# Gate outputs and three chunks of h transposed by 32x32 blocks on the vector engine, in a hybrid decoder layer

## The chip, the core and the metric

One core of a Trainium2 chip runs the whole layer as one program. The metric is device time in microseconds (us). The kernel before took 1821.63 us, the median of three runs (1821.47 to 1821.71). The engines are named as the profile names them: PE is TensorE (PEld its weight loads), DVE is VectorE, ACT is ScalarE, POOL is GpSimd, SP is SyncE, which only issues transfers here.

## The reference

A decoder layer over 256 tokens of width 2048, in fp32: a half-weighted SwiGLU feed-forward, a mixer of two head groups, a second feed-forward, a last norm.

```
h = x
h = h + 0.5 * swiglu(rmsnorm(h, ffn1_norm), w_gate, w_up, w_down)     # 2048 -> 5504 -> 2048
hn = rmsnorm(h, mix_norm);  q, k, v, u = split(hn @ w_in)
mixed = concat(rmsnorm(s5_mixer(u)), rmsnorm(dilated_attention(q, k, v)))
h = h + mixed @ w_out
h = h + 0.5 * swiglu(rmsnorm(h, ffn2_norm), w_gate, w_up, w_down)
return rmsnorm(h, final_norm)

swiglu(x) = (silu(x @ w_gate) * (x @ w_up)) @ w_down
```

## The kernel before

**Products.** Tokens lie on partitions, in two blocks of 128 (NTB = 2). Every product takes its left operand transposed (features on partitions, 256 tokens along the row) and its weights as they lie in memory. Both are kept as two fp32r halves, an upper one (the rounded value) and a lower one (the rest), and each product is the sum of three matmuls, xh*wh + xh*wl + xl*wh (mm3, L92 to L96, 128x512 each). `product` (L98) walks over the contraction in weight blocks of four k-tiles (1 MB, issued by SP, three buffers), and each block in two half blocks of two k-tiles: `halves` (L82) makes whi by a copy on ACT (L88) and wlo by a subtraction on DVE (L89), with four buffers of each, then 2 k-tiles x 2 token blocks x 3 matmuls follow. After each half block the next deferred closures of `self.soon` are called, and `step` (L175) draws one piece of background work from `self.later`. In the first feed-forward this is `prepare` (L627): tables of powers and of E for the state space, then eight groups (`ssm_groups`, L515), four yields each.

**Feed-forward.** `ffn` (L266) walks over 11 chunks of 512 columns (the last has 384): a gate product G, an up product U (8 half blocks each), then per token block a silu on ACT (L282), a product with U on DVE (L283, into one of two silu buffers), and a deferred `transpose_split` (L136): four 128x128 transposes on PE into PSUM (L142), a copy to the upper half on ACT (L146) and a subtraction for the lower half on DVE (L147). The result is a pair xh, xl that the down projection reads: four chunks of h, 22 half blocks each (L289 to L295).

**A finished chunk of h.** In the first feed-forward and in the second half of the mixer's output projection (L912 to L923, 4 half blocks for each chunk), `finish_chunk` (L250) defers the eight transposes of that chunk of h (with its gain, so that ACT and DVE split 128x128 pieces one by one, L151 and L152) and adds its squares to the statistics. The next product over h needs the pairs, one for each of its weight blocks.

**Start.** `setup` puts 12 matmuls on zeros in front (L203). The first gate product works in smaller pieces (`opening`, L104): x comes already transposed from memory and is split beside the weights (`split_x`, L229).

**End.** The last chunk of h is normed and stored (L931 to L945); `probe` (L947) issues 24 matmuls on zero tiles in between, whose results nobody reads.

**Order.** No queue is written out by hand. Tile's scheduler orders the instructions of each engine: the program's order is the priority, an instruction that is not ready by its plan is passed by others, and each engine then executes its list in the order so fixed. 32 slots of 4 KB per partition hold most tiles.

Of the kernel before, what the change touches and what calls it, by code (L numbers as in the profile page):

```python
# [4 lines left out]

# [4 lines left out]
F32 = mybir.dt.float32  # L10
F32R = mybir.dt.float32r
AF = mybir.ActivationFunctionType
# [19 lines left out]
class Layer:  # L32
# [4 lines left out]
    def __init__(self, ctx, tc, ins, out):  # L37
        self.tc, self.nc, self.t, self.out = tc, tc.nc, ins, out
        pool = lambda name, bufs, **kw: ctx.enter_context(tc.tile_pool(name=name, bufs=bufs, **kw))
        self.const = pool("const", 1)  # L40
        self.wpool = pool("weights", 2)
        self.slots = pool("slots", NSLOT)
        self.work = pool("work", 2)
        self.psum = pool("psum", 1, space=PSUM)
        self.dram = pool("scratch", 1, space=DRAM)
        self.n = 0
        self.later = deque()
        self.soon = deque()
        self.fetch = None


# [46 lines left out]
    def product(self, accs, xT, w, r0, nkt, c0, n, tail=0):  # L98


        held = []
        for k0 in range(0, nkt, 4):
            nk = min(4, nkt - k0)
            opening = self.fetch is not None and self.xraw is not None and k0 == 0  # L104
            raw = self.wraw(w, r0 + k0 * P, nk, c0, n, (1, 1, 2) if opening else (4,))
            if self.fetch is not None:
                self.fetch(k0 // 4 + 1)
            xh, xl = xT[k0 // 4]
            for kk, ke in ((0, 1), (1, 2), (2, 4)) if opening else ((0, 2), (2, 4)):
                ke = min(ke, nk)  # L110
                if kk >= ke:
                    continue
                if self.fetch is not None:
                    self.split_x(k0 + kk, k0 + ke)
                wh, wl = self.halves(raw[:, kk:ke, :n])
                for k in range(kk, ke):
                    for tb in range(NTB):
                        ts = slice(tb * P, (tb + 1) * P)
                        mm = partial(
                            self.mm3, accs[tb][:, :n], xh[:, k, ts], xl[:, k, ts], wh[:, k - kk, :n],  # L120
                            wl[:, k - kk, :n], k0 + k == 0, k0 + k == nkt - 1,
                        )
                        if tb and k0 + 4 * tail >= nkt:
                            held.append(mm)
                        else:
                            mm()
                while self.soon and k0 + kk >= 2:
                    self.soon.popleft()()
                self.step()
        for mm in held:  # L130
            mm()
# [4 lines left out]
    def transpose_split(self, pair, src, tb, nt, gain=None):  # L136

        nc = self.nc
        hi, lo = pair
        ps = self.trp()  # L140
        for k in range(nt):
            nc.tensor.transpose(ps[:, k * P : (k + 1) * P], src[:, k * P : (k + 1) * P], self.ident)  # L142
        ts = slice(tb * P, (tb + 1) * P)
        if gain is None:
            psv = ps[:, : nt * P].rearrange("p (k t) -> p k t", t=P)
            nc.scalar.activation(hi[:, :nt, ts], psv, AF.Copy)  # L146
            nc.vector.tensor_sub(lo[:, :nt, ts], psv, hi[:, :nt, ts].bitcast(F32))  # L147
        else:
            for k in range(nt):
                pk = ps[:, k * P : (k + 1) * P]  # L150
                nc.scalar.activation(hi[:, k, ts], pk, AF.Copy, scale=gain[:, k : k + 1])  # L151
                nc.vector.scalar_tensor_tensor(  # L152
                    lo[:, k, ts], pk, gain[:, k : k + 1], hi[:, k, ts].bitcast(F32),
                    op0=ALU.mult, op1=ALU.subtract,
                )

    def stat(self, nchunk):
        return [
# [29 lines left out]
    def setup(self):  # L188
        nc, t = self.nc, self.t
        self.gains = self.const.tile([P, 64], F32, name="gains")  # L190
        nc.scalar.dma_start(self.gains, t["gains"])
        self.g_ffn1, self.g_mix, self.g_ffn2 = (self.gains[:, 16 * i : 16 * i + 16] for i in range(3))
        self.g_ssm, self.g_att = (self.gains[:, 48 + 8 * i : 56 + 8 * i] for i in range(2))
        self.h = self.const.tile([P, NTB, D_MODEL], F32, name="h")
        self.ident = self.const.tile([P, P], F32, name="ident")
        self.even = self.const.tile([P, 3], F32, name="even")
        self.mhalf = self.even[:, 2:3]

        warm = self.slot([P, 512], F32R, s="warm")
        nc.vector.memset(warm.bitcast(F32), 0.0)  # L200
        idle = self.acc("idle")
        for _ in range(12):
            nc.tensor.matmul(idle, warm[:, :P], warm, start=True, stop=True)  # L203
        self.xraw = {}
        self.xT = [None] * 4
        self.st = self.stat(4)

        def fetch(c):
            if c == 2 and self.xraw is None:
                for tb in range(NTB):  # L210
                    nc.sync.dma_start(self.h[:, tb], t["x"][tb])
                nc.gpsimd.dma_start(self.ident, t["mask"][:, 3 * P : 4 * P])
                nc.gpsimd.dma_start(self.even, t["mask"][:, 4 * P :])
                self.later.appendleft(self.first_squares())
            if c > 3 or self.xT[c] is not None:
                return
            self.xraw[c] = raw = self.slot([P, 4, SEQ], s="xraw")
            self.xT[c] = self.pair()
            if c:
                self.fetch_x(c, 0, 4)  # L220

        self.r = None
        self.fetch = fetch
        fetch(0)
# [25 lines left out]
    def finish_chunk(self, c, gain):  # L250

        self.xT[c] = pair = self.pair()
        hs = [self.h[:, tb, c * 512 : (c + 1) * 512] for tb in range(NTB)]

        def transposes():
            for tb in range(NTB):
                self.transpose_split(pair, hs[tb], tb, 4, gain[:, 4 * c : 4 * c + 4])

        self.soon.append(transposes)
        for tb in range(NTB):  # L260
            self.square(self.st[tb], c, hs[tb], 512)

# [3 lines left out]
    def ffn(self, wg, wu, wd, finish, tail=0):  # L266
        nc = self.nc
        gT = []
        for c0, n in FCH:
            G = [self.acc("g") for _ in range(NTB)]  # L270
            self.product(G, self.xT, wg, 0, 16, c0, n)
            self.xraw = None
            U = [self.acc("u") for _ in range(NTB)]
            self.product(U, self.xT, wu, 0, 16, c0, n)
            if self.fetch is not None:
                self.fetch = None
                self.norms()
            pair = self.pair()
            gT.append(pair)
            for tb in range(NTB):  # L280
                s = self.tmp([P, 512], "silu", 2)
                nc.scalar.activation(s[:, :n], G[tb][:, :n], AF.Silu, scale=self.r[tb])  # L282
                nc.vector.scalar_tensor_tensor(  # L283
                    s[:, :n], U[tb][:, :n], self.r[tb], s[:, :n], op0=ALU.mult, op1=ALU.mult
                )
                self.soon.append(partial(self.transpose_split, pair, s, tb, n // P))
        self.xT = [None] * 4
        self.st = self.stat(4)
        for c in range(4):  # L289
# [636 lines left out]
    def ffn2(self):  # L926
# [1 line left out]
        self.gfin = None  # L928
        self.ffn(t["ffn2_w_gate"][0], t["ffn2_w_up"][0], t["ffn2_w_down"][0], self.last_chunk, 2)
        out = self.out  # L930
        self.probe()  # L931
        for tb in range(NTB):
            r = self.tmp([P, 1], "rstd", 6)
            nc.vector.tensor_scalar(r, self.st[tb][:, 3:4], 1.0 / D_MODEL, self.part[tb], op0=ALU.mult, op1=ALU.add)
# [9 lines left out]
                    nc.scalar.activation(hs, hs, AF.Copy, scale=r)  # L944
                (nc.sync if c % 2 else nc.scalar).dma_start(out[tb, :, cs], hs)  # L945

    def probe(self):  # L947

        z, zb = self.idle
        mm = partial(self.nc.tensor.matmul, start=True, stop=True)  # L950
        p = [self.trp("idle") for _ in range(2)]
        for i in range(4):
            mm(p[0], z[:, :P], z)
        for i in range(4):
            mm(p[0], z[:, i * P : (i + 1) * P], z)
        for i in range(4):
            mm(p[0], zb[:, i * P : (i + 1) * P], zb[:, :512])
        for i in range(4):
            mm(p[0][:64], z[:, i * P : i * P + 64], z)
        for i in range(4):  # L960
            mm(p[i % 2], z[:, i * P : (i + 1) * P], z)
        for i in range(4):
            mm(p[0][:, :256], z[:, i * P : (i + 1) * P], z[:, :256])

    def last_chunk(self, c):
        nc = self.nc
        if c == 2:
            self.idle = self.slot([P, 512], F32R, s="z"), self.slot([P, 512], mybir.dt.bfloat16, s="zb")
            nc.gpsimd.memset(self.idle[0].bitcast(F32), 0.0)
            nc.gpsimd.memset(self.idle[1], 0.0)  # L970
        if self.gfin is None:
            gf = self.t["final_norm"].rearrange("(o d) -> o d", o=1)
            self.gfin = [self.slot([P, 512], s="gfin") for _ in range(4)]
# [83 lines left out]
```

## Time and profile before

| | |
|---|---|
| median of three runs | 1821.63 us |
| the profiled execution | 1820.6 us |
| its span, first to last instruction | 1818.7 us |
| PE busy | 1810.3 us |
| DVE busy | 1033.5 us |
| ACT busy | 862.1 us |
| granted clock | 1.00 |

The profile is of one execution. Busy time is the union of the instructions of an engine; matmuls are pipelined, so that one of them shows about 390 ns while the next starts 227 ns later. A line of the timeline gives the start, the time that it covers, the engine, the line of the code, what is written from what, and in brackets the idle time before it and what ended it.

### The profile page before, as it was taken

What the parts mean: (1) busy time and instruction counts of PE and PEld (TensorE: products, weight loads), DVE (VectorE), ACT (ScalarE), POOL (GpSimd) and SP (SyncE); (2) the same over time, 40 slices, a digit from 0 to 9 for tenths busy, and PEclk for the clock granted to TensorE, in tenths of its full rate; (3) what the DMA queues carried; (4) which work ended last, traced back from release to release, by engine and by line L of the source; (5) the groups of instructions that cost most, each with busy time, mean ns of one, the idle gap of its engine ahead of it and who ended that gap; (6) DMA issues with size and microseconds to landing.
All of it is one profiled execution on the core that took longest, in us unless ns stands there. A gap on an engine that the chain in (4) does not pass through costs nothing.

```text
span 1818.7 us, 21868 instructions
## 1 busy us (share of the span) xinstructions
PE 1810.3 (100%) x8514; PEld 1519.8 (84%) x8515; DVE 1033.5 (57%) x1532; ACT 862.1 (47%) x1205; POOL 91.5 (5%) x175
## 2 busy tenths in 40 slices
PE   9999999999999999999999999999999999999999
PEld 7888888888988888888888888888888888988887
DVE  5796688545445544566666565544555544544553
ACT  6544567444444444443368555444444444444443
POOL 2102022500000000000000000000000000000000
PEclk9999999999999999999999999999999999999999
DMA  8667667855555557676544455555555555755553
GB/s 322 201 213 239 206 244 248 282 186 184 187 197 190 192 189 259 214 264 242 161 139 139 139 176 191 189 185 186 192 194 191 185 186 171 224 198 183 207 191 121
DMA packets 180327, 364.16 MB, mean 200 GB/s; under 512 B 8256, under 2 KB 17344, under 8 KB 179968
## 3 DMA queue, kind: packets, MB, share of 16 engines
q1 hardware_dynamic: 172192, 343.96, 56.6%
q0 software_dynamic: 6736, 16.69, 2.7%
q10 hardware_dynamic: 1296, 2.13, 0.4%
q8 instruction: 66, 1.08, 0.2%
q14 instruction: 37, 0.30, 0.0%
HBM read 346.36 MB, written 16.38 MB: 199 GB/s over the span
## 4 chain that ended last, share of the span: by engine, by line
PE 99%; DMA 1%; SPq 0%; DVE 0%; ACT 0%; issue 0%
PE u L94 9%; PE u L96 9%; PE y L96 9%; PE u L95 9%; PE y L95 9%; PE y L94 9%; PE g L95 9%; PE g L96 9%; PE g L94 8%; PE pr L94 3%; PE pr L96 3%; PE pr L95 3%; PE tr L142 2%; PE wo L94 2%; PE wo L96 2%; PE wo L95 2%
## 5 line engine op out<-in xcount | busy, mean ns | idle before, releaser
L89 DVE TENSOR_TENSOR wlo<-wraw,whi 128x1024 fp32r<-128x1024 f32 (+2 forms) x633 | 760.3, 1203 | 715.1 <-ACT whi L88 714.2
L88 ACT ACTIVATE whi<-wraw 128x1024 fp32r<-128x1024 f32 (+2 forms) x633 | 659.1, 1043 | 845.3 <-PE y L96 258.0
L94 PE MATMUL g<-whi,xh 128*128 128x512 f32 (+1 forms) x704 | 272.6, 388 | 2.0 <-ACT xh L237 1.5
L95 PE MATMUL g<-wlo,xh 128*128 128x512 f32 (+1 forms) x704 | 270.8, 385 | 1.1 <-DVE wlo L89 1.1
L94 PE MATMUL u<-whi,xh 128*128 128x512 f32 (+1 forms) x704 | 270.7, 385 | 0.0
L96 PE MATMUL g<-whi,xl 128*128 128x512 f32 (+1 forms) x704 | 270.5, 385 | 0.0
L96 PE MATMUL u<-whi,xl 128*128 128x512 f32 (+1 forms) x704 | 270.4, 384 | 0.0
L95 PE MATMUL u<-wlo,xh 128*128 128x512 f32 (+1 forms) x704 | 270.3, 384 | 0.0
L94 PE MATMUL y<-whi,xh 128*128 128x512 f32 x688 | 268.1, 390 | 0.0
L96 PE MATMUL y<-whi,xl 128*128 128x512 f32 x688 | 267.7, 389 | 0.0
L95 PE MATMUL y<-wlo,xh 128*128 128x512 f32 x688 | 267.7, 389 | 0.0
L94 PEld LDWEIGHTS g<-whi,xh 128*128 128x128 f32 x704 | 132.0, 188 | 27.8 <-ACT xh L237 2.2
L95 PEld LDWEIGHTS g<-wlo,xh 128*128 128x128 f32 x704 | 132.2, 188 | 26.3 <-DVE wlo L89 1.9
L96 PEld LDWEIGHTS g<-whi,xl 128*128 128x128 f32 x704 | 132.1, 188 | 25.0
L95 PEld LDWEIGHTS u<-wlo,xh 128*128 128x128 f32 x704 | 132.2, 188 | 24.9
L96 PEld LDWEIGHTS u<-whi,xl 128*128 128x128 f32 x704 | 132.1, 188 | 25.0
L94 PEld LDWEIGHTS u<-whi,xh 128*128 128x128 f32 x704 | 132.1, 188 | 24.8
L95 PEld LDWEIGHTS y<-wlo,xh 128*128 128x128 f32 x688 | 129.2, 188 | 26.9
L96 PEld LDWEIGHTS y<-whi,xl 128*128 128x128 f32 x688 | 129.1, 188 | 26.7
L94 PEld LDWEIGHTS y<-whi,xh 128*128 128x128 f32 x688 | 129.1, 188 | 26.6
L94 PE MATMUL pr<-whi,xh 128*128 128x512 f32 x256 | 101.9, 398 | 0.0
L96 PE MATMUL pr<-whi,xl 128*128 128x512 f32 x256 | 100.2, 391 | 0.0
(221 smaller groups left out, 1450.1 us busy)
## 6 DMA issues: line engine op xcount, KB each, us to landing
wraw<-in_ffn_w_up SPq DMA_DIRECT2D x80, 1024.0 KB, 5.1
wraw<-in_ffn_w_down SPq DMA_DIRECT2D x80, 1024.0 KB, 5.0
wraw<-in_ffn_w_gate SPq DMA_DIRECT2D x79, 1024.0 KB, 5.1
wraw<-in_w_in SPq DMA_DIRECT2D x32, 1024.0 KB, 5.6
wraw<-in_w_out SPq DMA_DIRECT2D x16, 1024.0 KB, 5.0
wraw<-in_ffn_w_gate SPq DMA_DIRECT2D x8, 768.0 KB, 4.4
wraw<-in_ffn_w_up SPq DMA_DIRECT2D x8, 768.0 KB, 4.4
wraw<-in_ffn_w_down SPq DMA_DIRECT2D x8, 768.0 KB, 4.3
```

The source lines that it names most:

```text
L88: nc.scalar.activation(hi[:, :nk, :n], raw, AF.Copy)
L89: nc.vector.tensor_sub(lo[:, :nk, :n], raw, hi[:, :nk, :n].bitcast(F32))
L94: nc.tensor.matmul(out, xh, wh, start=first, stop=False)
L95: nc.tensor.matmul(out, xh, wl, start=False, stop=False)
L96: nc.tensor.matmul(out, xl, wh, start=False, stop=last)
L142: nc.tensor.transpose(ps[:, k * P : (k + 1) * P], src[:, k * P : (k + 1) * P], self.ident)
```

## The change

The transposes of all gate outputs and of the first three chunks of h (in both places that call `finish_chunk`) leave PE. `turn_split` takes a raw tile and defers 32 transposes on DVE: each takes 32 partitions of one token block, with four (three in the narrow chunk) 32x32 blocks along the row, and writes them turned to another group of 32 partitions. A last entry splits the whole into halves. `product` calls three entries of the list after each half block, and all that are left of a pair before the weight block that reads it. The first gate product is put under `manual_schedule`, so that its instructions are issued in the order written. The warm-up has 10 matmuls, the probe and its zero tiles go.

```diff
@@ product
+            while any(x is xT[k0 // 4] for x, _ in self.turns):
+                self.turns.popleft()[1]()
             xh, xl = xT[k0 // 4]
@@ product, after the matmuls of a half block
                 while self.soon and k0 + kk >= 2:
                     self.soon.popleft()()
+                for _ in range(min(3, len(self.turns))):
+                    self.turns.popleft()[1]()
                 self.step()
@@
+    def turn_split(self, pair, src, nt, gain=None):
+        nc = self.nc
+        hi, lo = pair
+        raw = self.slot([P, 4, SEQ], s="turned")
+
+        def turn(tb, a, b):
+            nc.vector.transpose(
+                raw[32 * b : 32 * b + 32, :nt, tb * P + 32 * a : tb * P + 32 * a + 32],
+                src[tb][32 * a : 32 * a + 32, : nt * P].rearrange("p (k q c) -> p q k c", q=4, c=32)[:, b],
+            )
+
+        def split():
+            if gain is None:
+                nc.scalar.activation(hi[:, :nt], raw[:, :nt], AF.Copy)
+                nc.vector.tensor_sub(lo[:, :nt], raw[:, :nt], hi[:, :nt].bitcast(F32))
+                return
+            for k in range(nt):
+                nc.scalar.activation(hi[:, k], raw[:, k], AF.Copy, scale=gain[:, k : k + 1])
+                nc.vector.scalar_tensor_tensor(
+                    lo[:, k], raw[:, k], gain[:, k : k + 1], hi[:, k].bitcast(F32), op0=ALU.mult, op1=ALU.subtract)
+
+        for tb in range(NTB):
+            for a in range(4):
+                for b in range(4):
+                    self.turns.append((pair, partial(turn, tb, a, b)))
+        self.turns.append((pair, split))
@@ setup
-        for _ in range(12):
+        for _ in range(10):
             nc.tensor.matmul(idle, warm[:, :P], warm, start=True, stop=True)
@@ finish_chunk
-        self.soon.append(transposes)
+        if c < 3:
+            self.turn_split(pair, hs, 4, gain[:, 4 * c : 4 * c + 4])
+        else:
+            self.soon.append(transposes)
@@ ffn
-            self.product(G, self.xT, wg, 0, 16, c0, n)
+            with self.tc.manual_schedule() if self.fetch is not None else nullcontext():
+                self.product(G, self.xT, wg, 0, 16, c0, n)
@@
-            for tb in range(NTB):
-                s = self.tmp([P, 512], "silu", 2)
+            src = [self.tmp([P, 512], "silu", 2) for _ in range(NTB)]
+            for tb, s in enumerate(src):
...
-                self.soon.append(partial(self.transpose_split, pair, s, tb, n // P))
+            self.turn_split(pair, src, n // P)
@@ ffn2, last_chunk
-        self.probe()
...
-            self.idle = self.slot([P, 512], F32R, s="z"), self.slot([P, 512], mybir.dt.bfloat16, s="zb")
-            nc.gpsimd.memset(self.idle[0].bitcast(F32), 0.0)
-            nc.gpsimd.memset(self.idle[1], 0.0)
```

## Rows read from the trace of the kernel before

**Rows 1.** The page, busy time of each engine, its share and instructions.

```profile
PE 1810.3 (100%) x8514; PEld 1519.8 (84%) x8515; DVE 1033.5 (57%) x1532; ACT 862.1 (47%) x1205; POOL 91.5 (5%) x175
```

**Rows 2.** Waits: who waited for whom, us in total, times, longest.

```profile
DVE wlo L89 <- ACT whi L88: 714.2, 519, 6.6
```

**Rows 3.** Timeline of ACT, a half block of the last down projection: start, us.

```profile
1784.07 1.06 ACT L88 ACTIVATE whi<-wraw 128x1024 fp32r<-128x1024 f32 x1 [1.66 <-PE y L96]
```

**Rows 4.** Chain in order of time: start, us, what; two transposes of gate chunks.

```profile
1146.68 0.87 PE tr L142 x8
1191.11 0.87 PE tr L142 x8
```

**Rows 5.** Timeline of DVE at a chunk's end in the second feed-forward.

```profile
1140.79 1.41 DVE L283 SCALAR_TENSOR_TENSOR silu<-u,rstd,silu 128x512 f32<-128x512 f32 x2
...
1145.08 1.23 DVE L89 TENSOR_TENSOR wlo<-wraw,whi 128x1024 fp32r<-128x1024 f32 x1 [1.49 <-ACT whi L88]
```

**Rows 6.** Line 142, the transposes on PE: count, ns, first and last start.

```profile
L142 PE MATMUL tr<-ident,silu x188: 270/272/273, 60.3 to 1581.1; 128*128 128x128 f32 x188
...
L142 PE MATMUL tr<-ident,h x64: 270/272/273, 565.0 to 1102.8; 128*128 128x128 f32 x64
```

**Rows 7.** Groups of DVE by form: busy us, mean ns, idle before.

```profile
L152 DVE SCALAR_TENSOR_TENSOR xl<-tr,gains,xh 128x128 fp32r<-128x128 f32 x96 | 30.1, 346 | 8.3 <-ACT xh L151 8.3
...
L542 DVE TENSOR_TENSOR tt<-pow,bb 128x128 f32<-128x128 f32 x64 | 14.6, 284 | 0.0
...
L842 DVE STREAM_TRANSPOSE u<-silu 128x512 f32<-128x512 f32 x4 | 2.8, 713 | 0.9 <-ACT silu L735 0.9
```

**Rows 8.** Timeline of DVE in the mixer: copies of half and of all partitions.

```profile
818.68 2.77 DVE L755 COPY qkT<-tr 64x512 f32<-64x512 f32 x4
...
849.85 1.29 DVE L755 COPY qkT<-tr 128x512 f32<-128x512 f32 x2 [0.84 <-PE tr L752]
```

**Rows 9.** Windows: us; busy PE, PEld, DVE, ACT, POOL; clock, DMA share, GB/s.

```profile
230.00:320.00 90.00, 90.00 (x449) 75.80 (x448) 73.58 (x187) 64.38 (x158) 19.41 (x33) 1.00 0.72 249
1062.40:1108.40 46.00, 46.00 (x220) 38.41 (x219) 32.01 (x57) 29.82 (x63) 1.06 (x2) 1.00 0.55 182
1140.00:1184.40 44.40, 44.40 (x202) 36.83 (x201) 22.11 (x21) 19.20 (x20) 0.00 (x0) 1.00 0.58 189
```

**Rows 10.** Windows, line 152 alone: us; busy DVE; clock, DMA share, GB/s.

```profile
1062.40:1108.40 46.00, 9.33 (x30) 1.00 0.55 182
```

**Rows 11.** Timeline of DVE: four splits, a late lower half, h chunk 0.

```profile
12.71 1.67 DVE L238 SCALAR_TENSOR_TENSOR xl<-xraw,gains,xh 128x256 fp32r<-128x256 f32 x4
...
311.07 1.22 DVE L89 TENSOR_TENSOR wlo<-wraw,whi 128x1024 fp32r<-128x1024 f32 x1
...
1061.00 1.40 DVE L921 SCALAR_TENSOR_TENSOR h<-wo,rstd,h 128x512 f32<-128x512 f32 x2
```

**Rows 12.** Timeline of POOL and PE: the tables' stores; that lower half's first matmul.

```profile
149.54 1.61 POOL L508 DMA_DIRECT2D sE<-E  x3
...
312.69 0.39 PE L95 MATMUL u<-wlo,xh 128*128 128x512 f32 x1
```

**Rows 13.** Timeline of the start: warm-up, first matmul, arrival of weights.

```profile
1.46 5.46 PE L203 MATMUL idle<-warm 128*128 128x512 f32 x12 [1.46 <-DVE warm L200]
...
8.42 0.50 PE L94 MATMUL g<-whi,xh 128*128 128x512 f32 x1 [1.50 <-ACT xh L237]
...
10.47 1.06 ACT L88 ACTIVATE whi<-wraw 128x1024 fp32r<-128x1024 f32 x1 [0.44 <-DMA wraw<-in_ffn_w_gate]
...
14.70 2.01 ACT L88 ACTIVATE whi<-wraw 128x1024 fp32r<-128x1024 f32 x2 [1.01 <-DMA wraw<-in_ffn_w_gate]
```

**Rows 14.** Timeline of the end: last store issued, last probe matmuls.

```profile
1813.70 0.34 ACTq L945 DMA_DIRECT2D out<-h  x1
...
1814.24 0.63 PE L963 MATMUL idle<-z 128*128 128x256 f32 x4
```

**Rows 15.** DMA issues by line: KB each, median us from issue to landing.

```profile
out<-h ACTq DMA_DIRECT2D x4, 256.0 KB, 3.2
```

More of the change, by code (lines that the diff above doesn't have):

```diff
@@ L2 @@
 from collections import deque
-from contextlib import ExitStack
+from contextlib import ExitStack, nullcontext
 from functools import partial
@@ L48, in __init__ @@
         self.soon = deque()
+        self.turns = deque()
         self.fetch = None
@@ L945, in ffn2 @@
                 (nc.sync if c % 2 else nc.scalar).dma_start(out[tb, :, cs], hs)
[L947 to L963, printed above, removed]
     def last_chunk(self, c):
         nc = self.nc
-        if c == 2:
-            self.idle = self.slot([P, 512], F32R, s="z"), self.slot([P, 512], mybir.dt.bfloat16, s="zb")
-            nc.gpsimd.memset(self.idle[0].bitcast(F32), 0.0)
-            nc.gpsimd.memset(self.idle[1], 0.0)
         if self.gfin is None:
```

## The prediction

> **What bounds the kernel now.** I read the page first: the tensor engine (PE) is busy for 1810.3 of 1818.7 us, the vector engine (DVE) for 57% [rows 1]. So an instruction taken off PE saves what it occupies there, as long as nothing else then makes PE wait. Next the waits: DVE's lower halves (wlo) wait for ScalarE's upper halves (whi) [rows 2], and those wait for PE to free a buffer [rows 3]. DVE is thus paced by PE and runs ahead of it by four buffers. How far ahead follows from the chunk pitch: two gate chunks of the second feed-forward start 44.43 us apart and hold 192 matmuls and eight transposes of 0.87 us together [rows 4], so a matmul takes (44.43 - 0.87) / 192 = 0.227 us and a half block of 12 takes 2.72 us. A freed buffer is refilled by 1.06 us of whi and 1.23 us of wlo [rows 3, 5], and PE comes to it three half blocks later: 8.16 - 2.3 = 5.9 us to spare. That is the cover under which DVE may fall behind before PE notices.
>
> **Part 1, the transposes that leave PE.** The chain has them at 0.87 us per eight, 0.109 us each [rows 4]. The source view counts 188 of silu tiles and 64 of h [rows 6]. Of the 188, 16 belong to the mixer's glu, which keeps them, so 172 go; of the 64, three chunks in four go in both places that call finish_chunk: 48. 220 x 0.109 = 24.0 us, all on the path: **-24.0 us**.
>
> **Part 2, what DVE gets for it.** Each set (a gate chunk or an h chunk) is 32 turns of 32 partitions x 128 elements. No such instruction is in the trace. The nearest in kind is the 128x512 block transpose with 713 ns; from a 128x128 operation (284 ns) to a 128x1024 one (1.23 us) the slope is 1.05 ns an element [rows 5, 7], so 384 elements fewer leave 713 - 403 = 310 ns. What counts is the distance between starts. Back to back, 64 operations of 128x128 fill 14.6 us, 0.228 us each: neighbours overlap. But four copies that alternate between two halves of the partitions take 2.77 us, 0.69 each, where the second of two whole ones adds only 1.29 - 0.69 = 0.60 [rows 8]: a change of start partition costs the overlap. Every turn writes to another partition block than the one before it. I take the full duration and 10 ns, 0.32 us a turn, bounds 0.228 (overlap kept) and 0.35 (the 346 ns of L152, the slowest of the 128x128 forms [rows 7]). A set then costs 32 x 0.32 = 10.2 us.
>
> The Trainium skill (VectorE: DVE Perf Modes, section "Two Vector instructions with no wait between them") gives this a rule: an instruction whose input or output starts in another group of 32 partitions than the last one's is held until all earlier ones have finished. The trace agrees for copies (0.69 against 0.60 us); for transposes no run shows it yet. With the rule the sum below stands, without it rival 1 does.
>
> *In a gate chunk far from everything else* there is room: DVE is busy for 22.1 of 44.4 us [rows 9], 10.2 more make 32.3. By the code three turns go into a half block: 1.23 + 0.96 = 2.2 of 2.72 us, and the 33 entries end in the eleventh of 16 half blocks. ScalarE's one wide split waits for the last turn with the next whi queued behind it, covered by the 5.9 us. A split of 1024 elements costs no more than the two of 512 that it replaces. The silu tiles are held longer, but their next writer comes a chunk later. The same holds in the down projection, 22 half blocks long. Cost 0; if the cover goes, rival 2.
>
> *In the output projection of the mixer* there is none. There a chunk of h lasts only four half blocks, three sets fall due within 33 us, and the second and third are forced out ahead of the first gate product's second and third quarter. From the end of h chunk 0 (1062.4) to that third quarter (1108.4 in the profile of before) lie 46.0 us, of which DVE works 32.0 [rows 9, 11]. Of that work 24 of the 30 L152 operations (9.33 us [rows 10]) disappear: 7.5 us; and PE is there 3 x 0.87 = 2.6 us earlier. Free: 46.0 - 2.6 - (32.0 - 7.5) = 18.9 us. Due: 96 turns, 30.7 us, and twelve scaled splits, four of which take 1.67 us [rows 11], 5.0 us: 35.7. Of the excess of 16.8 two lower halves for later blocks, 2.5 us, can be put off. PE waits **14.3 us**; bounds 5.5 (turns at 0.228) and 19.7 (0.35, nothing put off).
>
> *In the first feed-forward* DVE also prepares the state space tables. That work runs far ahead of its place in the code: the stores of the tables E go out at 149.5 us [rows 12], while the code's yields put them after 78 half blocks, about 222 us on PE's clock. It can be put off, and costs nothing. Not so the eight groups between 230 and 320 us, which PE paces, one per four half blocks: 73.6 of 90 us are busy, and already one lower half ends at 312.29 for a matmul at 312.69 [rows 9, 11, 12]. Two sets, 20.5 us, meet 16.4 us of free time: 4.1 over. The free time lies partly behind waits for ScalarE and is not all usable, so I take **8 us**; bounds 0 (the rest slides into the quieter time behind 320 us) and 20.5 (none usable). A gain is excluded, nothing is taken from DVE there.
>
> **Part 3, the first product in written order, ten warm-up matmuls for twelve.** PE starts at 8.42 us because ScalarE took the second weight block before the first x [rows 13]. In written order it starts when the warm-up ends, near 6.2. But the third and fourth block come by DMA at 10.47 and the next four at 14.70 [rows 13]; with PE at 12 matmuls per 2.72 us the early start is waited away there. In written order one matmul fewer slips in ahead of the wait for each lower half: **+0.2 us**, bounds -1.5 (the 1.50 us of idle time before 8.42) and +1.5 (the same lost again at 14.70). The x pieces now go ahead of the weights on SP's queue; the sum of bytes before block two is the same.
>
> **Part 4, the probe and its two zero tiles.** The last idle matmul ends at 1814.87, the last store is issued by 1814.04 and takes 3.2 us to land [rows 14, 15]: 1817.2, after the probe. **0 us**, bounds -0.6 and 0.
>
> **Part 5, the clock.** When PE waits 14 us in two pieces it may come back slower. The twelve warm-up matmuls, after an idle engine, take 5.46 us [rows 13], 2.7 more than 12 x 0.227, though the windows below show a granted clock of 1.00 [rows 9], and the matmuls after the idle 1.5 us at 8.42 run at full pace. Bounds 0 and 5.4 (two such returns); I take one in two of one, **+1.3 us**. The Trainium skill (TensorE: Matmul & The Clock Gate, "Part 1") says that an idle engine drops from 2.4 to 1.2 GHz; no stretch of this trace shows such a drop after work has begun.
>
> **Sum.** -24.0 + 14.3 + 8 + 0.2 + 0 + 1.3 = -0.2 us. The profiled execution took 1820.6 us (span 1818.7 and 1.9 around it) and stands 1.0 below the median of the runs; set against that median, 1821.63, the forecast is 1821.4 us, no change. About 0.2%, 3.6 us, is what a measurement of this kernel can tell from none.
>
> **Rival 1, DVE swallows it: faster.** The turns overlap at 0.228 us. Then the mixer's end costs 21.9 + 5.0 - 18.9 - 2.5 = 5.5 us, the two sets of the groups' stretch need 14.6 of 16.4 us, say 1, and the clock nothing: -24.0 + 5.5 + 1 + 0.2 = -17.3, **1804.3 us**. For it: all 128x128 rows overlap. Against it: the copies of [rows 8].
>
> **Rival 2, the turns come in bursts: slower.** The order on DVE is fixed ahead by a planner that fills gaps; it need not spread three per half block. DVE can take (2.72 - 1.23) / 0.32 = 4.6 turns per half block. At n it falls behind by 1.4 us (the two silu products [rows 5]) + 10.2 - 1.49 x 32 / n per set, and PE waits once that passes 5.9: above n = 8.4. At n = 10 it is 6.8 - 5.9 = 0.9 us in each of 21 chunks, 20 us: **1841 us**. For it: where DVE has preparation work, the rows of before show many operations between two lower halves. Against: below eight nothing happens.
>
> **Rival 3, it gives more back than it takes, in the two stretches named.** The upper bounds of both, 19.7 and 20.5, with one slow return: -24.0 + 19.7 + 20.5 + 2.7 + 0.2 = +19, 1840 us. Only part of this way is likely; it makes the upper end of the forecast's own range.
>
> **How the numbers follow.** The forecast's case (held turns, two stretches in which DVE sets the pace) gets 0.55, its own range is 1811 to 1834; within it the terms 14.3 and 8 are as likely too small as too large: faster 0.12, same 0.21, slower 0.22. Rival 1 gets 0.28, nearly all of it faster; rival 2 0.10; rival 3 0.07. Faster 0.39, same 0.22, slower 0.39. The range goes from 1803 (rival 1 and a little) to 1836 (most of the forecast's upper side); rival 2 and 3's ends, and a tail of rival 1, are left out.
>
> **What would show it.** Turns with starts 0.32 us apart (0.23 for rival 1). PE waiting for an xl or xh of h chunks 1 and 2 at the first gate product of the second feed-forward, 14 us in all, and for lower halves between 230 and 330 us, 8 us. A pitch of 43.56 us in later gate chunks, without idle time on PE (longer for rival 2). First gate matmul near 6.2 us, the up product starting where it did. Wrong I would be if the pitch is met but the waits at the mixer's end are missing, or if PE waits in every chunk.

## The result, and the profile after

The changed kernel takes **1839.9 us** (median, 1838.8 to 1840.7) beside 1821.7 for the kernel before on the same chip: a ratio of **1.0099 [1.0081, 1.0116]**, 18 us slower where 1821.4 and no change were forecast, and outside the range of 1803 to 1836. The spans of the two profiled executions differ by 1837.0 - 1818.7 = 18.3 us; the sums below are made against that.

The page of the changed kernel: span, busy times [rows 1], the group of turns, and the chain's shares.

```profile
span 1837.0 us, 22160 instructions
PE 1795.1 (98%) x8269; PEld 1495.0 (81%) x8269; DVE 1290.3 (70%) x2382; ACT 854.2 (47%) x1159; POOL 91.1 (5%) x173
PE 80%; DVE 16%; issue 2%; DMA 1%; ACT 1%; POOL 0%; SPq 0%; POOLq 0%; DVEq 0%; ACTq 0%
L170 DVE STREAM_TRANSPOSE turned<-silu 32x128 f32<-32x128 f32 (+1 forms) x704 | 210.9, 300 | 11.6
```

PE is busy 15 us less in a span that is 18 us longer. Its waits (who waited for whom: us in total, times, longest) say for whom:

```profile
PE g L96 <- DVE wlo L90: 13.7, 12, 4.1
PE g L95 <- ACT xh L181: 10.9, 2, 7.8
PE u L96 <- DVE wlo L90: 3.6, 6, 0.9
```

Where that happens is read from the start of each product, the first matmul that PE's timeline shows for it. The last columns are two kernels of the experiments below. A difference that grows down a column is time lost in that stretch, one that shrinks is time gained.

| product | before, us | changed | e1 | e2 | e3 |
|---|---|---|---|---|---|
| first gate | 8.42 | -2.7 | -2.5 | -3.0 | -2.5 |
| first up | 33.08 | -0.1 | +0.4 | -0.2 | +0.7 |
| third gate, chunk 2 | 99.78 | -0.7 | -0.2 | -0.3 | +0.7 |
| its up | 122.45 | +4.1 | +4.9 | -0.3 | +0.7 |
| sixth gate, chunk 5 | 234.44 | +8.5 | +8.6 | -0.3 | +0.7 |
| ninth gate, chunk 8 | 377.29 | +16.6 | +17.8 | -0.1 | +0.7 |
| first down projection | 500.34 | +14.4 | +15.6 | -0.1 | +0.3 |
| mixer's output projection | 992.56 | +11.0 | +12.2 | -2.9 | -3.1 |
| second feed-forward, first gate | 1096.64 | +8.3 | +12.2 | -5.6 | -3.1 |
| its up | 1119.31 | +27.5 | +12.2 | +13.4 | -3.1 |
| end of the span | 1818.69 | +18.3 | +3.0 | +4.2 | -12.3 |

(Chunks are counted from 0.) Three stretches lose. **Chunks 2 to 4**, where the tables are prepared. DVE's timeline (start, us, line, what) behind the silu products of chunk 1:

```profile
103.11 1.22 DVE L90 TENSOR_TENSOR wlo<-wraw,whi 128x1024 fp32r<-128x1024 f32 x1
104.25 1.40 DVE L321 SCALAR_TENSOR_TENSOR silu<-u,rstd,silu 128x512 f32<-128x512 f32 x2
105.56 0.92 DVE L170 STREAM_TRANSPOSE turned<-silu 32x128 f32<-32x128 f32 x3
106.50 0.69 DVE L364 TENSOR_TENSOR tb<-par,b 128x512 f32<-128x512 f32 x1
107.20 0.93 DVE L170 STREAM_TRANSPOSE turned<-silu 32x128 f32<-32x128 f32 x3
108.15 0.69 DVE L364 TENSOR_TENSOR tb<-par,b 128x512 f32<-128x512 f32 x1
108.87 0.93 DVE L170 STREAM_TRANSPOSE turned<-silu 32x128 f32<-32x128 f32 x3
109.84 0.69 DVE L364 TENSOR_TENSOR bb<-tb 128x512 f32<-128x512 f32 x1
110.45 1.22 DVE L90 TENSOR_TENSOR wlo<-wraw,whi 128x1024 fp32r<-128x1024 f32 x1
```

There is no gap in it: nine turns, three products of the preparation and two silu products stand between two lower halves, whose starts are 7.3 us apart where PE wants one every 2.72. The same moment on PE:

```profile
107.24 0.39 PE L95 MATMUL g<-whi,xh 128*128 128x512 f32 x1
111.72 0.80 PE L96 MATMUL g<-wlo,xh 128*128 128x512 f32 x1 [4.09 <-DVE wlo L90]
112.31 0.63 PE L97 MATMUL g<-whi,xl 128*128 128x512 f32 x1
...
114.78 0.39 PE L97 MATMUL g<-whi,xl 128*128 128x512 f32 x1
```

**Chunks 5 to 7**, the groups' stretch: chunks 5 and 6 lose in eight waits of 0.3 to 1.0 us for lower halves, chunk 7 in one of 2.27 us. Ahead of that one DVE, with the next lower half behind it in its list, stood idle for 4.98 us until a transfer for the tables had come (DVE, then PE):

```profile
348.91 1.29 DVE L653 TENSOR_TENSOR dm<-ident,d 32x512 f32<-32x512 f32 x2 [4.98 <-DMA d<-in_ssm_d]
```

```profile
358.07 0.50 PE L96 MATMUL g<-wlo,xh 128*128 128x512 f32 x1 [2.27 <-DVE wlo L90]
```

**The first gate product of the second feed-forward** loses most, where the turns of the third chunk of h are forced out in one row ahead of the weight block that needs them (DVE, then PE):

```profile
1124.21 8.22 DVE L170 STREAM_TRANSPOSE turned<-h 32x128 f32<-32x128 f32 x26
1132.46 1.23 DVE L90 TENSOR_TENSOR wlo<-wraw,whi 128x1024 fp32r<-128x1024 f32 x1
```

```profile
1117.43 0.50 PE L95 MATMUL g<-whi,xh 128*128 128x512 f32 x1 [3.05 <-ACT xh L181]
...
1133.03 0.79 PE L95 MATMUL g<-whi,xh 128*128 128x512 f32 x1 [7.83 <-ACT xh L181]
...
1138.57 0.43 PE L95 MATMUL g<-whi,xh 128*128 128x512 f32 x1
```

The windows (us; busy PE, PEld, DVE, ACT, POOL; granted clock, DMA share, GB/s) show the same three, then two returns from waits, then an ordinary gate chunk, which loses nothing:

```profile
100.00:150.00 50.00, 45.59 (x194) 37.04 (x193) 48.61 (x157) 21.26 (x28) 4.32 (x8) 0.97 0.59 194
230.00:320.00 90.00, 86.55 (x416) 70.44 (x415) 85.64 (x229) 61.42 (x145) 17.06 (x31) 1.00 0.74 251
1109.00:1150.00 41.00, 28.43 (x106) 21.51 (x107) 30.16 (x71) 17.83 (x32) 2.00 (x2) 0.83 0.39 128
112.30:114.50 2.20, 2.20 (x7) 1.72 (x6) 2.11 (x5) 0.00 (x0) 0.00 (x0) 0.50 0.77 190
1133.00:1138.20 5.20, 5.17 (x12) 3.69 (x13) 3.41 (x6) 1.17 (x3) 0.00 (x0) 0.50 0.09 13
1168.50:1212.00 43.50, 43.50 (x193) 36.02 (x193) 31.27 (x52) 19.07 (x19) 0.00 (x0) 1.00 0.59 192
```

### The profile page after: what moved, and what is told of

The parts are those of the page before. It is cut to its first block, busy times and chain, and to the rows that moved or that the text cites. A ratio compares the mean times of both kernels' runs of the same rounds, so it can differ in the third digit from the quotient of the medians.

```text
span 1837.0 us, 22160 instructions
## 1 busy us (share of the span) xinstructions
PE 1795.1 (98%) x8269; PEld 1495.0 (81%) x8269; DVE 1290.3 (70%) x2382; ACT 854.2 (47%) x1159; POOL 91.1 (5%) x173
## 4 chain that ended last, share of the span: by engine, by line
PE 80%; DVE 16%; issue 2%; DMA 1%; ACT 1%; POOL 0%; SPq 0%; POOLq 0%; DVEq 0%; ACTq 0%
PE y L97 9%; PE y L95 8%; PE y L96 8%; PE u L96 7%; PE u L97 7%; PE u L95 7%; DVE wlo L90 6%; PE g L97 6%; PE g L96 5%; PE g L95 5%; DVE turned L170 5%; PE pr L95 3%; PE pr L97 3%; PE pr L96 3%; DVE tt L580 1%
## 5 line engine op out<-in xcount | busy, mean ns | idle before, releaser
L96 PE MATMUL g<-wlo,xh 128*128 128x512 f32 (+1 forms) x704 | 275.2, 391 | 14.1 <-DVE wlo L90 13.7
L170 DVE STREAM_TRANSPOSE turned<-silu 32x128 f32<-32x128 f32 (+1 forms) x704 | 210.9, 300 | 11.6
```

Of the source, the lines that this page charges most:

```text
L96: nc.tensor.matmul(out, xh, wl, start=False, stop=False)
L170: nc.vector.transpose(raw[32 * b : 32 * b + 32, :nt, tb * P + 32 * a : tb * P + 32 * a + 32], src[tb][32 * a : 32 * a + 32, : nt * P].rear ...
```

## The experiments

Twelve kernels ran, each timed beside the kernel before on the same chip. The theory (A in the texts): VectorE is where the time goes, and only in stretches where it has too little room for the turns between two lower halves; each stretch loses by itself. The rivals: the loss belongs to the planner's order as a whole and moves elsewhere, or it comes from bursts rather than from the amount of work.

### One stretch at a time: e1, e2, e3

e1 gives the mixer's h back to PE, e2 the gate outputs of the first feed-forward, e3 both (but for its last gate output).

```diff
# e1
-        if c < 3:
+        if c < 3 and gain is self.g_mix:
             self.turn_split(pair, hs, 4, gain[:, 4 * c : 4 * c + 4])
# e2 (e3: e1, and here "if tail or len(gT) > 9:")
-            self.turn_split(pair, src, n // P)
+            if tail:
+                self.turn_split(pair, src, n // P)
+            else:
+                for tb, s in enumerate(src):
+                    self.soon.append(partial(self.transpose_split, pair, s, tb, n // P))
```

> The changed kernel, but the three chunks of h at the mixer's end go through TensorE again as before (those of FFN1 and all gate outputs stay turned). Theory A (VectorE sets the pace where it is already full; the places lose separately): the first gate product of FFN2 no longer grows by 19 us against the kernel before, and the 24 transposes of 0.109 us (2.6 us) come back ahead of it; 1839.9 - 19.2 + 2.7 = about 1823.4, and the 32x128 turns fall from 704 to 608. Rival B (the loss is not of this place: it comes from the order that the planner gives to the whole kernel, or from the clock, and moves elsewhere): within 5 us of 1839.9, and the lost time shows in other products.

> The changed kernel, but FFN1's gate outputs go through TensorE again as before (FFN2's gate outputs and all six chunks of h stay turned). Theory A: FFN1 from its third product on has its old starts again up to the start of its down product; the 14.4 us that were lost there go, 1839.9 - 14.4 = about 1825.5, give or take 2. Rival B (the loss moves, or it comes from the preparation's DMAs and not from the turns): 1835 or more, with waits of TensorE for lower halves between 100 and 400 us as in the changed kernel.

> The changed kernel with turns left only where VectorE has idle time: FFN2's gate outputs, the last gate output of FFN1 and FFN1's three chunks of h; the rest through TensorE as before. Theory A, if the two places add up: 1839.9 - 16.5 - 14.4 = about 1809, that is 1821.7 less the transposes saved in FFN2 (86 of 0.109 us = 9.4) and in FFN1's end (2 to 4 of 0.109 x 12 chunks' worth, about 3 us), so 1808 to 1811, ratio to before 0.9925 to 0.994. Rival B (the loss moves with the planner's order): 1815 or more.

Measured: e1 1823.4 us (1.0016 [1.0006, 1.0025]), e2 1825.5 (1.0026 [1.0015, 1.0036]), e3 **1807.4** (0.9927 [0.9912, 0.9942]). e1 and e2 fall where theory A put them; e3 lies 1.6 us below its 1809 and 0.6 below its range. The table above shows each stretch losing by itself: in e1 nothing is lost behind the mixer and the first feed-forward loses as in the changed kernel, in e2 the reverse. In e3 PE's waits for lower halves are down to one:

```profile
PE g L96 <- DVE wlo L90: 0.8, 1, 0.8
```

So the gain on PE was real. The rival of a loss that moves is out.

### The start alone: e4

The kernel before with the written order of the first product and ten warm-up matmuls; nothing turned, the probe kept.

```diff
-        for _ in range(12):
+        for _ in range(10):
...
+            with self.tc.manual_schedule() if self.fetch is not None else nullcontext():
-            self.product(G, self.xT, wg, 0, 16, c0, n)
+                self.product(G, self.xT, wg, 0, 16, c0, n)
```

> The kernel before with the first gate product issued in written order and 10 warm-up matmuls in place of 12; nothing is turned, and the probe behind the last product stays. The prediction on record put the start at +0.2 us (-1.5 to +1.5) and the probe at 0; by the trace of the changed kernel, whose first up product starts 0.12 us earlier, the start is worth -0.1 and the whole is within 0.5 us of the kernel before.

Measured 1821.6 us, 1.0003 [0.9994, 1.0012]: no difference. In its trace the first gate product starts 2.9 us earlier and the first up product 0.5 us later.

### Half as many, longer turns: e5

```diff
-        def turn(tb, a, b):
+        def turn(a, b):
             nc.vector.transpose(
-                raw[32 * b : 32 * b + 32, :nt, tb * P + 32 * a : tb * P + 32 * a + 32],
-                src[tb][32 * a : 32 * a + 32, : nt * P].rearrange("p (k q c) -> p q k c", q=4, c=32)[:, b],
+                raw[32 * b : 32 * b + 32, :nt].rearrange("p k (t q c) -> p q t k c", q=4, c=32)[:, a],
+                src[32 * a : 32 * a + 32, :, : nt * P].rearrange("p t (k q c) -> p q t k c", q=4, c=32)[:, b],
             )
...
-        for tb in range(NTB):
-            for a in range(4):
-                for b in range(4):
-                    self.turns.append((pair, partial(turn, tb, a, b)))
+        for a in range(4):
+            for b in range(4):
+                self.turns.append((pair, partial(turn, a, b)))
...
-            src = [self.tmp([P, 512], "silu", 2) for _ in range(NTB)]
+            src = self.slot([P, NTB, 512], s="silu")
```

> The changed kernel with 16 turns of 32x256 (both time blocks in one instruction) in place of 32 of 32x128 for each set; same data moved. The price of a 32x256 turn isn't known: between 0.30 us (all fixed) and 0.63 us (all per element); with the size of the vector instructions of the trace of before as guide about 0.45. Theory A (the turns' time on VectorE is what is lost): a set falls from 10.1 us to 16 x 0.45 = 7.2, 30% less, and the 33 us lost in the two places falls by roughly that share, to about 1830. If the price is 0.63, no change (1838 to 1841). Rival B (order, not VectorE's time, loses it: lower halves stand behind whole bursts): the loss stays within 3 us of the changed kernel even if a set gets shorter.

Measured **1814.8 us**, 0.9969 [0.9957, 0.9981]: faster than the changed kernel and the kernel before with every turn still on DVE, 15 us below theory A's 1830 and further below rival B's.

```profile
L170 DVE STREAM_TRANSPOSE turned<-silu 32x256 f32<-32x256 f32 x320 | 139.5, 436 | 6.1 <-issue 0.5
```

The price was right (436 ns; starts 448 ns apart, so a set takes 7.2 us). The step from it was wrong: 30% less DVE work took 25 of the changed kernel's some 42 us of loss away, 60%. The loss is not a share of the work; it is what is left after the free time and the halves in hand are used up, so the first microseconds saved count most. At the mixer's end that can be added up: the prediction's sum for that place gives with 48 turns of 0.448 us 21.5 + 5.0 - 18.9 - 2.5 = 5.1 us, and e5 loses 2.5 us between the output projection and the first up product although 2.6 us of transposes are saved there, 5.1. Some 4 of the 25 us are the clock, whose granted value stays at 1.00 there in e5 (1095 to 1150 us). The silu tiles, which e5 keeps in other buffers, are no rival of weight: in the changed kernel writers of silu wait for turns 1.7 us in all.

### The same work, issued more thinly: e7, e8

```diff
# e7, on e5 (e8, on the changed kernel: min(2, ...))
-                for _ in range(min(3, len(self.turns))):
+                for _ in range(min(1, len(self.turns))):
```

> The kernel with 16 turns of 32x256 a set everywhere, but one turn a half block is issued in place of three (the last of a set come with the next product that needs them). Same VectorE work. Theory A (VectorE is full in the stretches that lose): within 3 us of 1814.8, with the lower halves of the third up product and of FFN2's first gate product as late as before. Rival B (bursts of nine turns of 0.45 us, 4 us at a time, hold up lower halves that would otherwise be in time): the 4.4 us lost at the third up product and the 3.8 us at FFN2's first gate product go, 1808 or less.

> The changed kernel with two turns a half block in place of three (same 32 turns of 32x128 a set, same VectorE work; bursts of six in place of nine). Theory A: within 4 us of 1839.9, the third up product still 3 us or more later than in the kernel before. Rival B (the bursts): 1832 or less, and the third up product starts within 1.5 us of the kernel before.

Measured: e7 1811.4 us (0.9949 [0.9934, 0.9964]), 3.5 below e5; e8 1835.9 us (1.0082 [1.0065, 1.0098]), 4.0 below the changed kernel. e8 keeps to theory A, by a hair; e7 lies between the two. The starts against before (those of the changed kernel stand in the first table):

| product | e5 | e7 | e8 |
|---|---|---|---|
| up of chunk 2 | +4.4 | -1.3 | +3.3 |
| gate of chunk 5 | +2.6 | +0.7 | +10.4 |
| first down projection | +6.0 | -4.5 | +11.3 |
| mixer's output projection | +2.6 | -7.9 | +7.9 |
| second feed-forward, its first up | +5.1 | +0.4 | +24.6 |

With sets of 7.2 us it was the burst alone that cost time in the groups' stretch: spread (e7), six sets bring their 0.87 us each there (+0.7 to -4.5), where e5 loses 6.0 - 2.6 + 5.2 = 8.6. With sets of 10.1 us the loss there is 14.4 - 8.5 + 6 x 0.87 = 11.1 us in the changed kernel and 11.3 - 10.4 + 5.2 = 6.1 in e8: issued more thinly, about half of it goes. Whether the other half is lack of room or the bursts of six that are left was not tried. Where DVE is full, from 100 us on, spreading moves the wait (e7: -1.3 at chunk 2's up product, +1.6 at chunk 3's) and lessens it less: from chunk 2's to chunk 5's gate product the starts fall back by 3.6 us in e5 and by 2.1 in e7. And at the mixer's end it does harm: with fewer turns issued early, more are forced out in one row (12 ahead of the last weight block that needs them, 5 in e5), and from the output projection to the first up product e7 loses 8.3 us, e5 2.5. The waits of e7 that are longest:

```profile
PE g L95 <- ACT xh L181: 6.6, 2, 5.4
```

### Twice the turns where there was room: e9

e3 with each turn of the second feed-forward's gate outputs done twice.

```diff
+          for _ in range(2 if gain is None and hasattr(self, "gfin") else 1):
             nc.vector.transpose(
```

> The kernel with both places back on TensorE (1807.4), but every turn of FFN2's gate outputs is done twice: 352 more instructions of 0.316 us, 10.1 us more VectorE time in each of FFN2's eleven gate chunks of 43.5 us. Theory A: VectorE is busy 31 to 36 of each 43.5 us there, so 10.1 more fills it; what TensorE loses is what a burst of 18 turns (5.7 us) outlasts the halves in hand, 0 to 2 us a chunk: 1807 to 1829, and a wait of TensorE for the lower half behind each burst if it is above 1812. Rival B (VectorE's work in FFN2 is covered whatever its size as long as the sum fits): 1807.4 within 2 us.

Measured 1846.9 us, 1.0144 [1.0129, 1.0159]: 39.5 us over e3 and beyond the bounds given: the gate chunks are 46.7 us apart in place of 43.5, 3.2 lost in each. Over a whole chunk there was room, and PE lost all the same: the window (DVE busy 44.15 of 50 us), DVE's timeline, which shows the reason, and PE's waits.

```profile
1200.00:1250.00 50.00, 48.70 (x206) 37.59 (x205) 44.15 (x91) 19.89 (x20) 0.00 (x0) 1.00 0.55 188
```

```profile
1224.01 1.23 DVE L90 TENSOR_TENSOR wlo<-wraw,whi 128x1024 fp32r<-128x1024 f32 x1 [0.71 <-ACT whi L89]
...
1229.45 1.23 DVE L90 TENSOR_TENSOR wlo<-wraw,whi 128x1024 fp32r<-128x1024 f32 x1 [1.50 <-ACT whi L89]
1230.59 1.41 DVE L322 SCALAR_TENSOR_TENSOR silu<-u,rstd,silu 128x512 f32<-128x512 f32 x2
1231.91 5.48 DVE L171 STREAM_TRANSPOSE turned<-silu 32x128 f32<-32x128 f32 x17
1237.42 1.23 DVE L90 TENSOR_TENSOR wlo<-wraw,whi 128x1024 fp32r<-128x1024 f32 x1
1238.68 1.92 DVE L171 STREAM_TRANSPOSE turned<-silu 32x128 f32<-32x128 f32 x6
1240.63 1.23 DVE L90 TENSOR_TENSOR wlo<-wraw,whi 128x1024 fp32r<-128x1024 f32 x1
...
1243.85 1.23 DVE L90 TENSOR_TENSOR wlo<-wraw,whi 128x1024 fp32r<-128x1024 f32 x1
```

```profile
PE g L96 <- DVE wlo L90: 9.7, 34, 0.8
PE u L96 <- DVE wlo L90: 6.2, 27, 0.6
```

The lower half at 1229.45 us is still in step with PE. The next one starts 7.97 us later where PE takes 2.72, so DVE is 5.2 us behind, and a half block with six turns takes DVE 3.21 us, so it falls behind by 0.5 more at each: 5.7, then 6.2 at 1243.85. The spare of the prediction is 5.9 us, and that third lower half is the first that PE waits for:

```profile
1245.13 0.50 PE L96 MATMUL g<-wlo,xh 128*128 128x512 f32 x1 [0.22 <-DVE wlo L90]
```

From there PE waits at every half block with turns, 59 short waits in the second feed-forward, and the free time behind them (DVE waits for ACT from 1218 us on) comes too late to be used. What has to fit into the spare is what DVE falls behind over the row of half blocks that carry turns; free time in the chunk as a whole does not tell that.

### Put together: e6, e10, e11, e12

All use e5's turns. e6 turns FFN1's gate outputs but for 1, 5, 6, 7; e10 is e7 with the mixer's h on PE; e11 is e10 with FFN1's gate outputs 1 and 2 on PE too; e12 is e10 with the first of the mixer's three chunks of h turned.

```diff
# e10, e11
-        if c < 3:
+        if c < 3 and gain is self.g_mix:
# e12
+        if c < (3 if gain is self.g_mix else 1):
# e6 (and e1's line); e11: (1, 2)
+            if tail or len(gT) - 1 not in (1, 5, 6, 7):
```

> Both findings together: 16 turns of 32x256 a set (436 ns each in the run before) and turns only where VectorE has room: FFN2's gate outputs, FFN1's chunks of h and FFN1's gate outputs 0, 2, 3, 4, 8, 9 and 10; FFN1's gate outputs 1, 5, 6 and 7 (behind them lie the table's preparation and the groups) and h at the mixer's end through TensorE. Theory A: each of the six further sets saves 8 transposes of 0.109 us, 0.9 us, if VectorE carries 7.2 us more in those chunks: 1807.4 - 5.4 = 1802.0; where a set does not fit its 0.9 us is lost again, so 1801 to 1807. Rival B (any turns in FFN1's first 400 us move the planner's order and stall TensorE): above 1810.

> Turns of 32x256, one a half block, for all 22 gate sets and FFN1's three chunks of h; the mixer's three chunks of h through TensorE as before. Theory A (half blocks whose VectorE work stays below TensorE's 2.72 us cost nothing, and the rest of the loss was at the mixer's end): the run before it with the mixer's h on TensorE stands 7.9 us ahead of the kernel before at the mixer's output projection, keeps that to FFN2's first up product and gains 9.4 in FFN2: 1820.8 - 17.3 = about 1803.5 (1802 to 1806). Rival B (the first product of FFN2 still waits, since FFN1's spread sets or the planner's order moved): above 1808.

> As the kernel with one 32x256 turn a half block and the mixer's h on TensorE, and FFN1's gate outputs 1 and 2 on TensorE too: their chunks are those in which the preparation of the table keeps VectorE 96% busy. Theory A: 3.0 us of waits at the third and fourth gate and up products go and 1.8 us of transposes come back, 1.2 us ahead of that kernel: about 1802.3. Rival B (they are free when spread): 1.8 us slower than it, about 1805.3.

> As the kernel with one 32x256 turn a half block and the mixer's h on TensorE, but the first of the mixer's three chunks of h is turned. Theory A (FFN2's first gate product is held up because three sets and their splits have to be through before a fixed place; the first one has 26 us before it): 0.9 us saved, so 0.9 us faster within 0.6. Rival B (the set itself doesn't fit beside the mixer's end): 2 us or more slower, with a wait of TensorE in FFN2's first gate product.

| kernel | us, median | ratio to before |
|---|---|---|
| e6 | 1805.6 | 0.9916 [0.9901, 0.9931] |
| e10 | 1802.8 | 0.9902 [0.9888, 0.9916] |
| e11 | **1801.4** | 0.9893 [0.9879, 0.9907] |
| e12 | 1801.8 | 0.9896 [0.9880, 0.9912] |

e6 came out 3.6 us above its likeliest value, inside its bounds; its trace has a wait of 1.25 us behind chunk 4's set and one of 0.70 behind chunk 2's. e10 to e12 came within 1 us of the forecasts. The medians of these three differ by no more than their intervals; their traces part them. Up to the down projection e11 stands at -7.8 us against e10's -5.0 (the two sets that meet the preparation cost more than they save), and between the mixer's output projection and the second feed-forward's first up product e12 gains 0.9 us where e10 gains nothing: one set of h is free there, so it is the second and third that don't fit. Which of those two, and whether one of them alone would fit, was not tried. e11 is 20 us faster than before, 38 faster than the change.

## Why the prediction was wrong

Its sum was -24.0 + 14.3 + 8 + 0.2 + 0 + 1.3 = -0.2. By the trace of the changed kernel it should have read, in the order of the points below, -24.0 + 10.6 + 5.7 + 10.7 + 14.9 - 0.1 + 0.4 = +18.2, against the spans' 18.3 (the 0.4: behind chunk 8's gate product three sets bring 2.2 of their 2.6 us).

- **"It can be put off, and costs nothing"** (the tables' preparation): this step failed, and it holds 10.6 of the missing 18.4 us (the clock holds 4.4, the groups 2.7, the mixer's end 0.6, the start -0.3, and 0.4 is named above). From the first up to chunk 5's gate product the changed kernel loses 8.5 + 0.1, and the four sets saved there should have brought 4 x 0.87 = 3.5: 12.1 lost, 1.5 of it slow matmuls. The work was indeed put off: the stores of the tables, which ran from 137.7 to 151.2 us (the row of [rows 12] is one of them), now run from 176.8 to 188.0. But on DVE it lies in a list with the lower halves, and a lower half behind it waits as long as it does. Due dates of the work itself don't matter in such a list. The sets that meet the preparation are what costs: from chunk 2's to chunk 5's gate product e5 loses 3.6 us and three sets' 2.6, e6, which has only chunk 1's set back on PE there, 0.9 in all, and e11, with chunks 1's and 2's back and the rest spread, nothing. One window of the kernel before would have priced this and is missing in the sum: DVE was already busy for 48.05 of 50 us there. Under it the first store of that kernel, then that of the changed one.

```profile
100.00:150.00 50.00, 50.00 (x228) 41.47 (x227) 48.05 (x138) 23.78 (x31) 11.75 (x22) 1.00 0.72 241
```

```profile
137.73 2.14 POOL L508 DMA_DIRECT2D sE<-E  x4 [25.08 <-DVE E L326]
```

```profile
176.80 2.13 POOL L546 DMA_DIRECT2D sE<-E  x4 [71.27 <-DVE E L364]
```

- **Part 5, the clock**, "one in two of one, +1.3 us" (bounds 0 and 5.4): mis-sized, 5.7, just outside its bounds. Behind the waits of 4.09, 3.05 and 7.83 us the granted clock is 0.50, the level of 1.2 GHz (0.60 in the second window, whose first matmuls are still fast), and 7, 6 and 12 matmuls start 0.43 us apart or more: 3.06 - 7 x 0.227 = 1.5, 2.72 - 1.36 = 1.4, and from 1133.03 to 1138.57 5.54 - 2.72 = 2.8. That is what the prediction's sentence from the Trainium skill (TensorE: Matmul & The Clock Gate, "Part 1") says; the trace of before had not shown it, and this one does. The start has a fourth such stretch (granted clock 0.50 from 12.30 to 15.60 us), which costs nothing that the first up product shows: it starts at -0.1 us, and in e4, where the clock is 1.00 in that stretch, at +0.5.
- **The groups' stretch**, +8 (bounds 0 and 20.5): 10.7, from chunk 5's to chunk 8's gate product (16.6 - 8.5, and three sets of 0.87 that brought nothing). Up to chunk 7's gate product, which are the two sets that the prediction counted, it is 14.0 - 8.5 + 1.7 = 7.2: right. The other 3.5 us come from a third set that it had nothing for, where DVE stands still for 4.98 us for the table's transfer and nine turns then follow a lower half that is late already. In the kernel before DVE waits 3.41 us for that transfer and PE does not notice; nor does it in e7, with 3.7 us and the set spread. As cause the prediction had only lack of room; e7 and e8 show that bursts are a good part of it.
- **The mixer's end**, +14.3 (bounds 5.5 and 19.7): between the output projection and the first up product 16.5 us are lost and 24 transposes (2.6) saved, 19.1; less the 4.2 of slow matmuls there, 14.9. Right, and at the place named, with the waits for xh of chunks 1 and 2.
- **Part 1, -24.0**: right. e3, e10 and e11 show saved transposes as time wherever nothing waits, 0.90 us a chunk in the second feed-forward; the pitch there is 43.52 us (43.56 predicted).
- **Part 2's pace, 0.32 us a turn**: right. 26 turns in 8.22 us are 0.316 each at 303 ns a turn, so the next one starts only when the last is done. The rule of the Trainium skill (VectorE: DVE Perf Modes, "Two Vector instructions with no wait between them") agrees with that, for transposes too. The mixer's two block transposes of 128x512, which start on the same partition, do overlap: two of 713 ns take 1.39 us in the kernel before. That the change of partition alone is the reason is not shown: e9's repeated turns start on the same partitions as the ones before and are no closer (0.31 to 0.34 us), but they also write the same place. Either way rival 1, overlapped turns, is out.
- **Cover in an ordinary gate chunk, 0**: right, but not for the reason given. The turns do not come three to a half block. The planner put 9, 3, 5, 9 and 6 of them between lower halves, 6.4 on average:

```profile
1167.13 1.23 DVE L90 TENSOR_TENSOR wlo<-wraw,whi 128x1024 fp32r<-128x1024 f32 x1 [1.49 <-ACT whi L89]
...
1169.60 2.82 DVE L170 STREAM_TRANSPOSE turned<-silu 32x128 f32<-32x128 f32 x9
...
1184.70 1.23 DVE L90 TENSOR_TENSOR wlo<-wraw,whi 128x1024 fp32r<-128x1024 f32 x1
```

The fifth lower half starts 17.57 us after one that was in step, where PE takes 5 x 2.72, so DVE is 4.0 us behind, inside the 5.9. Rival 2's formula gives 1.4 + 10.2 - 1.49 x 32 / 6.4 = 4.15 for that: its premise, bursts, was right, its limit of 8.4 was not reached, and e9 shows its price once the limit of the spare is passed.
- **Start and probe, +0.2 and 0**: right within the measurement (-0.1 in the changed kernel; e4). e4 keeps the probe; that its removal brings nothing is read from the last down projection, whose start stands at +18.95 us and whose end at +18.28 in the changed kernel: 0.67 us, what its six transposes took. The first matmul comes at 5.68 us (near 6.2 predicted), and waits later give it back, as said.

Rival 3 named this outcome, "it gives more back than it takes", and its 1840 us. It reached it by the upper bounds of two stretches and one return of the clock; measured were the middle of both, a third stretch and three returns. So its number was luck in part.

## What to carry to other kernels

Work moved to an engine that feeds the busiest one is free only as long as what the feeder falls behind, added up from one delivery to the next and counted with everything else that is queued there, stays inside the spare that its buffers give (here 4.0 us of 5.9 cost nothing, 6.2 did); average idle time, even over one chunk, does not show it, and neither does a late due date of that other work. So read the feeder's busy time window by window, move the work only where there is room, spread it one piece per interval, and leave the old path where the consumer is due at once: here the same idea was +1.0% put everywhere, and -1.1% put where it fits, in longer turns and spread. Fewer, longer instructions come first: two turns in one cost 448 ns where two single ones cost 632.

## What the runs showed of the hardware that was not expected

- A turn's price has a large fixed part: 303 ns for 128 elements a partition, 436 for 256, so 170 ns and 1.04 ns an element; the 32x96 turns of the last chunks (269 ns) lie on the same line.
- Whether the clock is low behind a wait is not fixed by the length of the wait. In the changed kernel matmuls run at full pace after a wait of 2.29 us at 157 us and after 2.27 us at 355 us; in e1, whose timeline is the same there but 0.2 to 0.5 us later, a wait of 2.25 us is followed by seven matmuls 0.43 us apart, and so is the one of 2.29. The granted clock behind the second wait is 1.00 in the changed kernel and 0.50 in e1 (below, in that order, then e1's matmuls); e1 loses 3.7 us from chunk 7's to chunk 8's gate product, the changed kernel 2.6.

```profile
358.00:362.00 4.00, 3.92 (x17) 3.27 (x18) 3.82 (x9) 1.06 (x1) 4.00 (x8) 1.00 0.77 218
```

```profile
358.80:361.40 2.60, 2.60 (x8) 1.98 (x7) 2.48 (x6) 0.00 (x0) 2.60 (x6) 0.50 0.77 216
```

```profile
358.24 0.79 PE L96 MATMUL g<-wlo,xh 128*128 128x512 f32 x1 [2.25 <-DVE wlo L90]
358.83 0.63 PE L97 MATMUL g<-whi,xl 128*128 128x512 f32 x1
...
361.39 0.53 PE L97 MATMUL g<-whi,xl 128*128 128x512 f32 x1
```
